# Four pairs of k-tiles by seven products instead of three in a decoder block's gate/up groups, with the quarters on GpSimd's queue

## The chip, the cores and the metric

The kernel runs on one core of a Trainium2 chip. The metric is the device time of one execution in microseconds, the median of several runs.

## The reference

A block of 256 tokens and width 2048, in float32: a feed-forward half step, a mixer (gated DeltaNet beside stick-breaking attention), a second feed-forward half step, a gated input embedding, and a last norm.

```python
def swiglu(x, w_gu, w_down):
    gate, up = jnp.split(x @ w_gu, 2, axis=-1)
    return (jax.nn.silu(gate) * up) @ w_down

h = h + 0.5 * swiglu(rms_norm(h, ffn1_norm[i]), ffn1_w_gu[i], ffn1_w_down[i])   # D_FF = 5632
h = h + hybrid_mixer(rms_norm(h, mix_norm[i]), ...)
h = h + 0.5 * swiglu(rms_norm(h, ffn2_norm[i]), ffn2_w_gu[i], ffn2_w_down[i])
gate = jax.nn.sigmoid(rms_norm(h, ple_norm[i]) @ ple_w_gate[i])
h = h + gate * (p[i] @ ple_w_proj[i])
return rms_norm(h, final_norm)
```

## The kernel before

Every product of two float32 matrices is made of three matmuls: each operand is split into a high part (`xh`, `whi`) and a rest (`xl`, `wlo`), and xh whi + xh wlo + xl whi go into one PSUM bank. Weights come in pairs of k-tiles, 128 x 1024 values a load (`raw`). ScalarE casts `raw` to `whi`, VectorE subtracts to get `wlo`. `next_weights` splits two pairs and up to two sums ahead of use.

A feed-forward block (`ffn`) has 11 gate/up groups, each of 512 gate and 512 up columns over 16 k-tiles (8 pairs of k-tiles for each of two column blocks b, two token tiles t). After groups 3, 7 and 11 of them two down groups follow (of two column blocks each); these three stretches are the parts. A group's matmuls are of two kinds:

- Plain steps: one pair of k-tiles of one column block, 2 k-tiles x 2 token tiles x 3 = 12 matmuls.
- Seven products in the way of Strassen and Winograd. They take `ns` pairs of k-tiles of both column blocks together. Done plainly, one pair of k-tiles takes 2 x 12 = 24 matmuls; by seven products it takes 7 x 3 = 21. The weights of these k-tiles are the quarters `R` (k-tile j of every pair, column block b), 128 x 512 ns values each. Sums of them are built as they are used: ScalarE casts the present sum to `shi`, VectorE subtracts to `slo` (two buffers of each). The next sum is made by VectorE (two additions into `R` a group) or by an accumulating DMA from GpSimd's queue (two a group). The activations' own sums and their split (`S`, `Sh`, `Sl`) are made by `halves`, a pass for two pairs of k-tiles.

The first gate/up groups of a block (two in the first, one in the second) have plain steps alone. In all others `NS` = 3, and `NS_DOWN` = 2, 3, 3 for the three parts' down groups.

`plan` writes the order out: while a group's plain steps run, the seven products of the group behind it (its follower) stand between them at the steps `at`, in other PSUM banks, and the quarters of the group two further on are loaded into the buffers that the follower's sums set free:

```python
at = [first + j * (n_plain - 1 - first) // 7 for j in range(7)]
...
for x, one in zip((5, 6, 7, 7), after.loads()):
    loads.setdefault(at[x] if x < 7 else min(at[6] + 1, n_plain - 1), []).append(one)
```

All loads are issued on SP's queue, in the order of the plan, so one that waits for its buffer holds those behind it. At the end of a gate/up group VectorE multiplies (`sil`), transposes 32 x 32 blocks (`tb`), and `transposed` sends them through DRAM (`scr`) to `tT`, from which `hTh` and `hTl` are made. `lanes` advance such work by one `yield` at every plain step. A scheduler then fixes each engine's instruction order at build time.

Of the kernel before, what the change touches and what calls it, by code (L numbers as in the profile page):

```python
# [10 lines left out]
F32 = mybir.dt.float32  # L11
F32R = mybir.dt.float32r
# [4 lines left out]
P = 128  # L17
T = 256
# [11 lines left out]
NS = 3  # L30
# [11 lines left out]
def block_kernel(ctx, tc, a, out):  # L42
# [156 lines left out]
    def norm_block(nT, which, j, tmp):  # L199

        if j < 3:
            lanes.add(0, norm_block_behind(nT, which, j, tmp))
            return
# [39 lines left out]
    class Group:  # L243
# [24 lines left out]
        def load(self, j, b):  # L268

            self.raw[j, b] = raw = current[0].tile([P, NS, NB], F32, tag=f"R{j}{b}", name="R")[:, 0:self.ns]  # L270
            nc.sync.dma_start(out=raw, in_=self.quarters[b][j])
# [61 lines left out]
    def plan(n):  # L333
# [24 lines left out]
        made = []  # L358
        for i, group in enumerate(groups):
# [29 lines left out]
    for nb in range(3):  # L389
        order += [("pair", a["w_pp"][nb])] + [("pair", a["w_pg"][nb][g]) for g in range(KD // 2)]  # L390
    order.append(("pair", a["w_pp"][3]))

    def halves(kind, his, los, ns, wait=0):
# [5 lines left out]
        sh = fp.tile([P, 4, NS, P], F32R, tag="Sh", name="Sh")  # L399
        sl = fp.tile([P, 4, NS, P], F32R, tag="Sl", name="Sl")  # L400
        for g0 in range(0, ns, 2):
            n = min(2, ns - g0)
            hi, lo = his[g0 // 2], los[g0 // 2]
            x = fp.tile([P, 2, 4, P], F32, tag="tT", name="tT").rearrange("p t q y -> p (t q y)")[:, 0:2 * n * T]
            nc.vector.tensor_tensor(out=x, in0=hi[:, 0:2 * n].bitcast(F32).rearrange("p k x -> p (k x)"),
                                    in1=lo[:, 0:2 * n].bitcast(F32).rearrange("p k x -> p (k x)"), op=ALU.add)
            x = x.rearrange("p (g j t y) -> p g j t y", g=n, j=2, t=2)
            a11, a12, a21, a22 = (x[:, :, j, t, :] for t in range(2) for j in range(2))
# [870 lines left out]
```

## Time and profile before

| | us |
|---|---|
| runs | 1960.52, 1960.58, 1961.28 (median 1960.58) |
| the profiled execution | 1958.5 |
| its span | 1956.8 |
| TensorE, VectorE, ScalarE, GpSimd busy | 1939.7, 1536.0, 1153.7, 83.9 |

The profile is one execution; its span is what the hardware profiler saw of the program, and the execution's own time is a little longer. Matmuls overlap, and their ends are modelled, so how much TensorE does in a stretch is read from the distance between the starts of its matmuls. In rows of groups, "busy, mean ns of one | idle before" are given, with what ended that idle time.

### The profile page before, as it was taken

To read this page: it belongs to the slowest core of one execution; us is meant where nothing else is said; L and a number is where in the kernel's file an instruction comes from. 1 tells how busy PE (TensorE), PEld (TensorE's weight loads), DVE (VectorE), ACT (ScalarE), POOL (GpSimd) and SP (SyncE) were. 2 spreads that over 40 slices of the span, in tenths; PEclk is the share of its full clock that TensorE was granted. 3 is DMA by queue.
4 is the path that set the end of the run, shared out by engine and by line. 5 is a ranking of instruction groups with operands and counts; after the bars stand their busy time and mean duration, and the time that the engine had idled before them with its cause. 6 is when DMAs were issued, how large, how long until landed. Compare 5 with 4: busy or idle time off the path is not lost.

```text
span 1956.8 us, 24735 instructions
## 1 busy us (share of the span) xinstructions
PE 1939.7 (99%) x8945; PEld 1606.5 (82%) x8945; DVE 1536.0 (78%) x1771; ACT 1153.7 (59%) x1402; POOL 83.9 (4%) x108
## 2 busy tenths in 40 slices
PE   9999999999999999999999999999999999999998
PEld 7887888888888888878788888888888888888887
DVE  6889778897788766797856678888879887798755
ACT  7655656566565567664555465665566555665554
POOL 0000000000000000010100000000000000000000
PEclk9999999999999999999999999999999999999999
DMA  8988888888888765556555788887888878887764
GB/s 316 296 238 255 265 275 243 261 257 260 264 254 256 222 209 165 174 169 213 178 195 160 243 289 243 253 270 242 250 265 281 281 223 247 261 271 239 236 207 147
DMA packets 164379, 468.28 MB, mean 239 GB/s; under 512 B 20641, under 2 KB 59553, under 8 KB 164129
## 3 DMA queue, kind: packets, MB, share of 16 engines
q1 hardware_dynamic: 154176, 418.57, 62.1%
q0 software_dynamic: 8928, 46.67, 13.6%
q8 instruction: 70, 1.15, 0.2%
q10 hardware_dynamic: 1152, 1.47, 0.2%
q14 instruction: 53, 0.43, 0.1%
HBM read 444.62 MB, written 22.02 MB: 238 GB/s over the span
## 4 chain that ended last, share of the span: by engine, by line
PE 90%; DVE 5%; issue 3%; DMA 1%; ACT 1%; POOL 0%; SPq 0%; ACTq 0%; POOLq 0%; DVEq 0%
PE u L481 6%; PE u L482 6%; PE u L480 5%; PE g L480 5%; PE g L482 5%; PE g L481 5%; PE d L480 5%; PE d L482 5%; PE d L481 5%; PE pj L108 3%; PE pj L109 3%; PE pj L107 3%; PE g L316 3%; PE g L318 3%; PE g L317 3%
## 5 line engine op out<-in xcount | busy, mean ns | idle before, releaser
L72 ACT CAST whi<-raw 128x1024 fp32r<-128x1024 f32 (+1 forms) x531 | 557.0, 1051 | 525.3 <-PE d L482 113.6
L73 DVE TENSOR_TENSOR wlo<-raw,whi 128x1024 fp32r<-128x1024 f32 (+1 forms) x531 | 643.2, 1216 | 217.9 <-ACT whi L72 212.5
L285 DVE TENSOR_TENSOR slo<-R,shi 128x1536 fp32r<-128x1536 f32 (+1 forms) x217 | 365.6, 1686 | 125.1 <-ACT shi L284 123.5
L284 ACT CAST shi<-R 128x1536 fp32r<-128x1536 f32 (+1 forms) x217 | 309.7, 1428 | 158.6 <-PE g L318 50.6
L481 PE MATMUL u<-wlo,nTh 128*128 128x512 f32 x476 | 185.3, 389 | 0.2 <-DVE wlo L73 0.2
L481 PE MATMUL g<-wlo,nTh 128*128 128x512 f32 x476 | 185.4, 390 | 0.0
L482 PE MATMUL g<-whi,nTl 128*128 128x512 f32 x476 | 185.3, 389 | 0.0
L482 PE MATMUL u<-whi,nTl 128*128 128x512 f32 x476 | 185.2, 389 | 0.0
L480 PE MATMUL u<-whi,nTh 128*128 128x512 f32 x476 | 184.9, 389 | 0.0
L480 PE MATMUL g<-whi,nTh 128*128 128x512 f32 x476 | 184.3, 389 | 0.3 <-ACT whi L72 0.3
L107 PE MATMUL pj<-whi,nTh 128*128 128x512 f32 x448 | 179.6, 401 | 0.0
L108 PE MATMUL pj<-wlo,nTh 128*128 128x512 f32 x448 | 175.3, 391 | 2.2 <-DVE wlo L73 2.2
L109 PE MATMUL pj<-whi,nTl 128*128 128x512 f32 x448 | 174.9, 390 | 0.0
L481 PE MATMUL d<-wlo,hTh 128*128 128x512 f32 x448 | 174.3, 389 | 0.0
L480 PE MATMUL d<-whi,hTh 128*128 128x512 f32 x448 | 174.3, 389 | 0.0
L482 PE MATMUL d<-whi,hTl 128*128 128x512 f32 x448 | 174.3, 389 | 0.0
L289 DVE TENSOR_TENSOR R<-R 128x1536 f32<-128x1536 f32 (+1 forms) x62 | 104.4, 1684 | 0.9
L481 PEld LDWEIGHTS u<-wlo,nTh 128*128 128x128 f32 x476 | 89.3, 188 | 19.1 <-DVE wlo L73 0.7
L481 PEld LDWEIGHTS g<-wlo,nTh 128*128 128x128 f32 x476 | 89.4, 188 | 19.0 <-DVE wlo L73 0.4
L480 PEld LDWEIGHTS g<-whi,nTh 128*128 128x128 f32 x476 | 89.3, 188 | 18.9 <-ACT whi L72 0.5
L482 PEld LDWEIGHTS u<-whi,nTl 128*128 128x128 f32 x476 | 89.4, 188 | 18.6
L480 PEld LDWEIGHTS u<-whi,nTh 128*128 128x128 f32 x476 | 89.3, 188 | 18.6
(304 smaller groups left out, 3223.8 us busy)
## 6 DMA issues: line engine op xcount, KB each, us to landing
raw<-in_w_gu SPq DMA_DIRECT2D x237, 512.0 KB, 5.5
raw<-in_w_down SPq DMA_DIRECT2D x112, 512.0 KB, 5.2
raw<-in_w_in SPq DMA_DIRECT2D x112, 512.0 KB, 3.5
R<-in_w_gu2q SPq DMA_DIRECT2D x40, 768.0 KB, 5.9
R<-in_w_gu1q SPq DMA_DIRECT2D x36, 768.0 KB, 5.9
scr<-tb SPq DMA_DIRECT2D x74, 256.0 KB, 4.8
raw<-in_w_out SPq DMA_DIRECT2D x32, 512.0 KB, 4.6
raw<-in_w_pg SPq DMA_DIRECT2D x32, 512.0 KB, 4.1
```

The costliest lines, as they stand in the source:

```text
L72: nc.scalar.copy(hi[:, j, :], raw[:, j, :])
L73: nc.vector.tensor_tensor(out=lo[:, j, :], in0=raw[:, j, :], in1=hi[:, j, :], op=ALU.subtract)
L107: nc.tensor.matmul(outs[t], xh[:, c], whi[:, j, :], start=st, stop=False)
L108: nc.tensor.matmul(outs[t], xh[:, c], wlo[:, j, :], start=False, stop=False)
L109: nc.tensor.matmul(outs[t], xl[:, c], whi[:, j, :], start=False, stop=sp)
L284: nc.scalar.copy(hi, w)
L285: nc.vector.tensor_tensor(out=lo, in0=w, in1=hi, op=ALU.subtract)
L289: nc.vector.tensor_tensor(out=self.raw[x], in0=self.raw[x], in1=self.raw[y], op=ALU.add)
L316: nc.tensor.matmul(out, xh, whi[:, g, :], start=st, stop=False, skip_group_check=True)
L480: nc.tensor.matmul(out, xh[:, c], whi[:, j, :], start=st, stop=False, skip_group_check=True)
L481: nc.tensor.matmul(out, xh[:, c], wlo[:, j, :], start=False, stop=False, skip_group_check=True)
L482: nc.tensor.matmul(out, xl[:, c], whi[:, j, :], start=False, stop=sp, skip_group_check=True)
```

## The change

`NS` goes from 3 to 4: a gate/up group with products now has 8 plain steps instead of 10, and seven products of 12 matmuls instead of 9. The quarters grow from 768 to 1024 KB, and with them every cast, split, addition and accumulation of a gate/up sum. The down groups keep 2, 3, 3.

- `at` puts the products into neighbouring steps, from step 1 (gate/up after gate/up) or 2, and lets them pile up in the last step where a group has too few.
- The quarters of the group two further on are loaded from GpSimd's queue, in another order (the one that the first sum reads comes first, the last one in the next group's first step), each into the buffer that is free first. Only the first group's loads of a block stay on SP.
- `halves` works in place in the buffer of `sil`; a gate/up group has two passes of two pairs instead of one of two and one of one.
- The gated block goes through DRAM as one write of 512 KB and four reads in runs of 1 KB (two writes and four reads in runs of 512 B before), with more plain steps between write, reads and use.
- At a block's end the norm's blocks alternate between two lanes and two buffers.
- The input embedding is loaded and split in the last stage instead of ahead of the second feed-forward block, and its weights `w_pp` come after `w_pg`.

```diff
-NS = 3
+NS = 4
...
-            self.raw[j, b] = raw = current[0].tile([P, NS, NB], F32, tag=f"R{j}{b}", name="R")[:, 0:self.ns]
-            nc.sync.dma_start(out=raw, in_=self.quarters[b][j])
-
-        def loads(self):
-            return [("load", lambda j=j, b=b: self.load(j, b)) for j, b in ((0, 1), (1, 0), (0, 0), (1, 1))]
+            self.raw[j, b] = raw = current[0].tile([P, NS, NB], F32, tag=self.home[j, b], name="R")[:, 0:self.ns]
+            self.queue.dma_start(out=raw, in_=self.quarters[b][j])
+
+        def loads(self, last=None):
+            free = [last.home[q] for q in ((0, 1), (1, 0), (0, 0), (1, 1))] if last else ["R0", "R1", "R2", "R3"]
+            self.queue = nc.gpsimd if last else nc.sync
+            use = (0, 0), (0, 1), (1, 1), (1, 0)
+            self.home = dict(zip(use, free))
+            return [("load", lambda q=q: self.load(*q)) for q in use]
...
-            at, loads = [], {}
+            at, loads, carried = [], {0: carried}, []
             if follower is not None and follower.ns:
-                first = 2 if group.ns else 8
-                at = [first + j * (n_plain - 1 - first) // 7 for j in range(7)]
+                first = 8 if not group.ns else 1 if group.kind == follower.kind else 2
+                at = [min(first + j, n_plain - 1) for j in range(7)]
...
-                    for x, one in zip((5, 6, 7, 7), after.loads()):
-                        loads.setdefault(at[x] if x < 7 else min(at[6] + 1, n_plain - 1), []).append(one)
+                    *three, last = after.loads(follower)
+                    for x, one in zip((4, 5, 6), three):
+                        loads.setdefault(at[x], []).append(one)
+                    carried = [last]
...
-        order += [("pair", a["w_pp"][nb])] + [("pair", a["w_pg"][nb][g]) for g in range(KD // 2)]
+        order += [("pair", a["w_pg"][nb][g]) for g in range(KD // 2)] + [("pair", a["w_pp"][nb])]
...
-            x = fp.tile([P, 2, 4, P], F32, tag="tT", name="tT").rearrange("p t q y -> p (t q y)")[:, 0:2 * n * T]
+            x = fp.tile([P, 2 * NB], F32, tag="sil", name="S")[:, 0:n * NB]
...
-            def down_input(u, sil, th, tl):
+            def down_input(u, sil, th, tl, landing, back):
...
-                tT = fp.tile([P, 2, 4, P], F32, tag="tT", name="tT")
-                yield from transposed(lambda t: sil[:, t, :], tT)
+                tb = fp.tile([P, 4, 2, P], F32, tag="tT", name="tb")
+                for t in range(2):
+                    nc.vector.transpose(tb[:, :, t].rearrange("p c (j x) -> p c j x", j=4),
+                                        sil[:, t, :].rearrange("p (j c x) -> p c j x", j=4, c=4))
+                yield
+                scr = dr.tile([P, 4, 2, P], F32, tag="scr2", name="scr2", bufs=2)
+                nc.sync.dma_start(out=scr, in_=tb)
+                for _ in range(landing):
+                    yield
+                tT = fp.tile([P, 4, 2, P], F32, tag="tT", name="tT")
+                for c in range(4):
+                    nc.sync.dma_start(out=tT[32 * c:32 * c + 32].rearrange("x q t i -> x q (t i)"),
+                                      in_=scr[:, c].rearrange("(q x) t i -> x q (t i)", q=4))
+                for _ in range(back):
+                    yield
...
-                            norm_block(nxt, next_norm, nb, lambda: fp.tile([P, 2, 4, P], F32, tag="tT", name="tT"))
-                            lanes.advance(0)
+                            norm_block(nxt, next_norm, nb, lambda x=("tT", "sil")[nb % 2]:
+                                       fp.tile([P, 2, 4, P], F32, tag=x, name="tT"), nb % 2)
+                            lanes.advance(nb % 2)
```

What the scheduler makes of it, at three places. First GpSimd's queue in the first block's first part. Before, it holds the accumulations (L293) of one group after another:

```order
L293 DMA R<-in_w_gu1q 128x1536 x2
L293 DMA R<-in_w_down10q 128x1024 x4
L293 DMA R<-in_w_gu1q 128x1536 x8
L293 DMA R<-in_w_down11q 128x1536 x4
L293 DMA R<-in_w_gu1q 128x1536 x8
```

With the change the quarters' loads (L271) stand between the accumulations (L299):

```order
L299 DMA R<-in_w_gu1q 128x2048 x2
L271 DMA R<-in_w_down10q 128x1024 x4
L299 DMA R<-in_w_down10q 128x1024 x2
L271 DMA R<-in_w_down10q 128x1024 x4
L299 DMA R<-in_w_down10q 128x1024 x2
L271 DMA R<-in_w_gu1q 128x2048 x4
L299 DMA R<-in_w_gu1q 128x2048 x2
L271 DMA R<-in_w_gu1q 128x2048 x4
```

A group's four loads have come off SP's queue; they stand behind the accumulations of the group ahead of it and in front of its own.

Second VectorE from the first to the third split of a gate/up group that follows another (first block, second part). Before:

```order
L285 TENSOR_TENSOR slo<-R,shi 128x1536
L289 TENSOR_TENSOR R<-R 128x1536
L73 TENSOR_TENSOR wlo<-raw,whi 128x1024
L285 TENSOR_TENSOR slo<-R,shi 128x1536
L435 SCALAR_TENSOR_TENSOR sil<-u_3527,rstd_517,sil 128x512
L435 SCALAR_TENSOR_TENSOR sil<-u_3528,rstd_517,sil 128x512
L73 TENSOR_TENSOR wlo<-raw,whi 128x1024
L167 STREAM_TRANSPOSE tb<-sil 128x512 x2
L73 TENSOR_TENSOR wlo<-raw,whi 128x1024
L289 TENSOR_TENSOR R<-R 128x1536
L73 TENSOR_TENSOR wlo<-raw,whi 128x1024 x2
L285 TENSOR_TENSOR slo<-R,shi 128x1536
```

With the change:

```order
L291 TENSOR_TENSOR slo<-R,shi 128x2048
L445 SCALAR_TENSOR_TENSOR sil<-u_3429,rstd_515,sil 128x512
L295 TENSOR_TENSOR R<-R 128x2048
L445 SCALAR_TENSOR_TENSOR sil<-u_3430,rstd_515,sil 128x512
L73 TENSOR_TENSOR wlo<-raw,whi 128x1024
L452 STREAM_TRANSPOSE tb<-sil 128x4x128
L291 TENSOR_TENSOR slo<-R,shi 128x2048
L452 STREAM_TRANSPOSE tb<-sil 128x4x128
L295 TENSOR_TENSOR R<-R 128x2048
L73 TENSOR_TENSOR wlo<-raw,whi 128x1024 x2
L291 TENSOR_TENSOR slo<-R,shi 128x2048
```

The sums are wider, and three splits of pairs stand between the first and the third instead of five; the gating has come in between as before.

Third VectorE at the end of the first block's first part, where down goes over to gate/up and the halves of the gate/up activations are made. Before, from the first to the second pass:

```order
L289 TENSOR_TENSOR R<-R 128x1536
L414 TENSOR_TENSOR Sl<-S,Sh 128x4x256
L73 TENSOR_TENSOR wlo<-raw,whi 128x1024
L285 TENSOR_TENSOR slo<-R,shi 128x1536
L412 TENSOR_TENSOR S<-tT 128x128
L289 TENSOR_TENSOR R<-R 128x1536
L412 TENSOR_TENSOR S<-S,tT 128x128
L412 TENSOR_TENSOR S<-tT 128x128
L412 TENSOR_TENSOR S<-S,tT 128x128
L73 TENSOR_TENSOR wlo<-raw,whi 128x1024 x2
L414 TENSOR_TENSOR Sl<-S,Sh 128x4x128
L285 TENSOR_TENSOR slo<-R,shi 128x1536
```

With the change, the second pass:

```order
L295 TENSOR_TENSOR R<-R 128x2048
L431 TENSOR_TENSOR S<-S 128x2x128
L73 TENSOR_TENSOR wlo<-raw,whi 128x1024
L431 TENSOR_TENSOR S<-S 128x2x128
L73 TENSOR_TENSOR wlo<-raw,whi 128x1024
L431 TENSOR_TENSOR S<-S 128x2x128
L291 TENSOR_TENSOR slo<-R,shi 128x2048
L431 TENSOR_TENSOR S<-S 128x2x128
L516 SCALAR_TENSOR_TENSOR h<-d_1315,h 128x512
L516 SCALAR_TENSOR_TENSOR h<-d_1316,h 128x512
L73 TENSOR_TENSOR wlo<-raw,whi 128x1024
L434 TENSOR_TENSOR Sl<-S,Sh 128x1024
```

The second pass is as wide as the first, and the update of h has come in ahead of its end.

More of the change, by code (lines that the diff above doesn't have):

```diff
@@ L197, in norm_block_behind, with norm_block @@
                 yield
-    def norm_block(nT, which, j, tmp):
+    def norm_block(nT, which, j, tmp, lane=0):
         if j < 3:
-            lanes.add(0, norm_block_behind(nT, which, j, tmp))
+            lanes.add(lane, norm_block_behind(nT, which, j, tmp))
             return
@@ L357, in plan @@
             groups[0].plain.sort(key=lambda x: x[1])
-        made = []
+        made, carried = [], []
         for i, group in enumerate(groups):
@@ L509, in ffn @@
                         hTl.append(tl)
-                        gen = down_input(outs, sil, th, tl)
+                        i0, i1 = PARTS[group.part]
+                        last = len(hTh) == i1
+                        gen = down_input(outs, sil, th, tl, 2, (3 if i1 - i0 == 4 else 2) if last else 4)
                         next(gen)
                         lanes.add(0, gen)
-                        if len(hTh) == PARTS[group.part][1]:
+                        if last:
+                            lanes.advance(0)
                             lanes.advance(0)
```

57 lines of the change are left out of this document (30 added, 27 removed).

## The prediction

> **What bounds the kernel now.** I read the page's first part, then TensorE's own waits, then its spacing, since a kernel whose TensorE never waits is paid in matmuls.
>
> ```profile
> span 1956.8 us, 24735 instructions
> PE 1939.7 (99%) x8945; PEld 1606.5 (82%) x8945; DVE 1536.0 (78%) x1771; ACT 1153.7 (59%) x1402; POOL 83.9 (4%) x108
> ```
>
> ```profile
> PE pj L108 <- DVE wlo L73: 2.2, 4, 1.1
> PE u L316 <- ACT Sh L413: 1.3, 2, 0.9
> ```
>
> The page alone does not prove that TensorE is the bound, because the ends of its matmuls are modelled. Its waits do: their two largest rows (total, times, longest) are 2.2 and 1.3 us in a whole execution. The second one lies inside the feed-forward blocks, at the step from a part's down groups to the next gate/up group. What a matmul costs is the spacing of their starts. These are the first and the last of 32 neighbours ahead of that wait:
>
> ```profile
> 181.74 0.39 PE L481 MATMUL d<-wlo,hTh 128*128 128x512 f32 x1
> ...
> 188.76 0.39 PE L482 MATMUL d<-whi,hTl 128*128 128x512 f32 x1
> 190.04 0.50 PE L316 MATMUL u<-shi,Sh 128*128 128x512 f32 x1 [0.89 <-ACT Sh L413]
> ```
>
> (188.76 - 181.74)/31 = 0.2265 us a matmul, and then 0.89 us of waiting. VectorE is the engine next to the bound. The windows (length, then busy time and count of PE, PEld, DVE, ACT, POOL, then clock, DMA share, GB/s) hold one gate/up stretch (264 to 305.5), the two stretches with the wait, and one with much traffic:
>
> ```profile
> 150.00:200.00 50.00, 49.09 (x216) 39.90 (x215) 45.14 (x50) 30.83 (x34) 2.62 (x3) 1.00 0.81 243
> 264.00:305.50 41.50, 41.50 (x185) 34.37 (x184) 33.46 (x29) 25.07 (x26) 1.75 (x2) 1.00 0.86 268
> 1300.00:1350.00 50.00, 49.58 (x218) 40.29 (x217) 45.57 (x50) 30.96 (x34) 2.59 (x3) 1.00 0.81 246
> ```
>
> ```profile
> 200.00:250.00 50.00, 50.00 (x222) 41.40 (x221) 38.48 (x32) 30.10 (x29) 1.75 (x2) 1.00 0.86 282
> ```
>
> The granted clock is 1.00 in all of them. VectorE is busy 81% of a gate/up stretch, and 90% and 91% where TensorE loses 0.9 and 0.4 us.
>
> **TensorE.** Taking one more pair of k-tiles through the products replaces 2 plain steps of 12 matmuls (24) by 3 more matmuls in each of 7 products (21). That holds for 9 + 10 = 19 gate/up groups, so 19 x 3 = 57 matmuls go: 57 x 0.2265 = 12.9 us. All of it lies on the path. The down groups keep their numbers.
>
> **VectorE and ScalarE.** What the splits, sums and halves cost is in the groups by form:
>
> ```profile
> L73 DVE TENSOR_TENSOR wlo<-raw,whi 128x1024 fp32r<-128x1024 f32 x529 | 641.8, 1218 | 216.4 <-ACT whi L72 211.2 <-DMA tT<-scr 1.5 <-DMA raw<-in_w_down 1.5
> L285 DVE TENSOR_TENSOR slo<-R,shi 128x1536 fp32r<-128x1536 f32 x189 | 331.6, 1755 | 121.5 <-ACT shi L284 121.1
> L289 DVE TENSOR_TENSOR R<-R 128x1536 f32<-128x1536 f32 x54 | 94.7, 1753 | 0.8
> L285 DVE TENSOR_TENSOR slo<-R,shi 128x1024 fp32r<-128x1024 f32 x28 | 34.0, 1221 | 3.7 <-ACT shi L284 2.4
> ...
> L491 DVE SCALAR_TENSOR_TENSOR h<-d,h 128x512 f32<-128x512 f32 x48 | 31.1, 682 | 3.5 <-PE d L482 3.5
> L435 DVE SCALAR_TENSOR_TENSOR sil<-u,rstd,sil 128x512 f32<-128x512 f32 x44 | 30.9, 743 | 0.0
> L167 DVE STREAM_TRANSPOSE tb<-sil 128x512 f32<-128x512 f32 x44 | 28.6, 686 | 0.0
> L444 DVE TENSOR_TENSOR hTl<-tT,hTh 128x512 fp32r<-128x512 f32 x44 | 28.3, 684 | 0.0
> L324 DVE TENSOR_TENSOR g<-g,part 128x512 f32<-128x512 f32 x38 | 26.3, 693 | 3.5 <-ACT part L323 3.5
> ...
> L414 DVE TENSOR_TENSOR Sl<-S,Sh 128x1024 fp32r<-128x1024 f32 x12 | 14.6, 1220 | 1.4 <-ACT Sh L413 1.4
> ...
> L412 DVE TENSOR_TENSOR S<-S,tT 128x256 f32<-128x256 f32 x24 | 10.0, 417 | 0.1
> ...
> L405 DVE TENSOR_TENSOR tT<-nTh,nTl 128x1024 f32<-128x1024 f32 x6 | 7.3, 1224 | 0.2
> ...
> L414 DVE TENSOR_TENSOR Sl<-S,Sh 128x512 fp32r<-128x512 f32 x10 | 6.8, 682 | 0.0
> L412 DVE TENSOR_TENSOR S<-S,tT 128x128 f32<-128x128 f32 x20 | 5.7, 283 | 0.0
> ...
> L405 DVE TENSOR_TENSOR tT<-nTh,nTl 128x512 f32<-128x512 f32 x6 | 4.1, 684 | 0.0
> ```
>
> ```profile
> L284 ACT CAST shi<-R 128x1536 fp32r<-128x1536 f32 x189 | 280.4, 1484 | 152.4 <-PE g L318 48.6 <-DVE R L289 37.3 <-PE d L318 21.9
> L284 ACT CAST shi<-R 128x1024 fp32r<-128x1024 f32 x28 | 29.3, 1056 | 6.2 <-PE d L318 4.3 <-PE g L318 2.0
> ```
>
> 512 columns more cost 1755 - 1221 = 0.534 us on VectorE and 1484 - 1056 = 0.428 on ScalarE, so a split of 2048 columns is estimated at 2.29 us, its cast at 1.91, and an addition R at 2.29. Three rows cost 0.69: the additions in PSUM (L324), the transposes and the splits of the gated block; h costs 0.68.
>
> Gate/up following gate/up (13 stretches), before: 10 pairs x 1.218 + 7 splits x 1.755 + 2 additions R x 1.753 + 4 x 0.69 in PSUM + 2 x 0.743 for the gating + 4 x 0.69 for its transposes and splits = 35.0 us, while TensorE takes 183 x 0.2265 = 41.4. The window's 33.5 confirms it (neighbours overlap a little). After: 8 x 1.218 + 9 x 2.29 + 7.0 = 37.4 us against 180 x 0.2265 = 40.8, that is 92% instead of 84%. TensorE still covers it.
>
> Down to gate/up at the second part (two stretches, one in each block), before: 12.2 + 12.3 + 3.5 + 2.8 + 2.7 for h + 6.6 for the halves (one pass of 1.22 + 4 x 0.417 + 1.22 = 4.1, one of 0.68 + 4 x 0.283 + 0.68 = 2.5) = 40.1 against 41.4. After, with both halves' passes at 4.1: 46.5 against 204 x 0.2265 = 46.2. At the first part (two stretches, 8 plain steps): 37.6 against 36.0 before, 44.1 against 40.8 after. This is where TensorE lost the 0.9 and 0.4 us. The excess doubles from 1.6 to 3.3 us, but the products now stand in steps 2 to 7 instead of 2, 2, 3, 4, 4, 5, 6: the one that waited for the halves comes a plain step (2.7 us) later. Bounds: from -1.3 (both waits vanish) to +3.4 (each grows by the 1.7 us more). I take 0, since the later step and the larger excess nearly cancel. For the two second-part stretches I take 0.3 us each, with 0 and 0.9 (the nearest wait that the trace has) as ends: 0.6.
>
> Elsewhere the lead of the splits over the products decides. A split in a gate/up stretch, and the first product matmul that reads it:
>
> ```profile
> 448.20 1.76 DVE L285 TENSOR_TENSOR slo<-R,shi 128x1536 fp32r<-128x1536 f32 x1 [0.56 <-ACT shi L284]
> ```
>
> ```profile
> 453.22 0.39 PE L317 MATMUL g<-slo,nTh 128*128 128x512 f32 x1
> ```
>
> It is ready 3.3 us ahead (453.22 - 449.96). There are two buffers, so a cast starts when the product two before it ends. From there to its own product are now 3 more matmuls (0.68 us), and cast and split take 0.43 + 0.53 longer: the lead falls by 0.3 to 3.0 us. So no wait in the steady stretch: 0, with 0 to 0.4 each as bounds (0 to 5.2). The place with the smallest lead is the first block's third product, where the sums begin:
>
> ```profile
> 68.76 1.76 DVE L285 TENSOR_TENSOR slo<-R,shi 128x1536 fp32r<-128x1536 f32 x1 [1.60 <-ACT shi L284]
> ```
>
> ```profile
> 70.83 0.39 PE L317 MATMUL g<-slo,Sh 128*128 128x512 f32 x1
> ```
>
> Its lead is 0.3 us (70.83 - 70.52). Three sums of 2048 columns take 3 x 0.96 + 2 x 0.53 = 3.9 us more, and two longer products give back 1.4, so the worst is 2.2. The quarter that the first sum reads is now loaded first instead of third, which can cancel it. Between 0 and 2.2 I take 0.7.
>
> **Transfers.** The queues, the issues and SP's waits:
>
> ```profile
> q1 hardware_dynamic: 154176, 418.57, 62.1%
> q0 software_dynamic: 8928, 46.67, 13.6%
> ```
>
> ```profile
> R<-in_w_gu2q SPq DMA_DIRECT2D x40, 768.0 KB, 5.9
> R<-in_w_gu2q POOLq DMA_DIRECT2D x20, 768.0 KB, 8.3
> ```
>
> ```profile
> SPq L271 <- DVE slo L285: 293.4, 111, 4.8
> ```
>
> ```profile
> L293 POOL DMA_DIRECT2D R<-in_w_gu2q x20: 862/865/947, 1175.1 to 1709.4; - x20
> ```
>
> SP sat 293 us behind quarters whose buffers were not free, and the pairs behind them in its queue sat too. 116 quarters leave it for GpSimd's queue, which now holds four loads and two accumulations for each group, 6 x 0.87 = 5.2 us of issuing in 40.8. SP's gain is worth nothing now, as none of TensorE's waits above ends with a transfer. On GpSimd's queue the accumulations now stand behind quarters that wait for a buffer; each of these buffers is freed by a split that precedes the accumulation's own cause on VectorE, so nothing is held: 0. An accumulation of 1 MB should land after 8.3 x 4/3 = 11 us; three products, 16.3 us, lie between its issue and its use.
>
> The gated block's way through DRAM becomes one write and four reads instead of two and four, with pieces twice as long, and has two steps more. It is read only by the last four plain steps of the down group: 0. The input embedding's split (one 512-column cast and subtraction) moves to the last stage, where VectorE is the less loaded:
>
> ```profile
> 1850.00:1900.00 50.00, 49.59 (x219) 40.73 (x219) 29.71 (x36) 26.92 (x36) 0.71 (x1) 1.00 0.65 217
> ```
>
> 30 of 50 us: 0, and putting w_pg ahead of w_pp gives at most the 0.4 us lost here.
>
> **Sum.** The profiled execution took 1958.5 us, a span of 1956.8 and 1.7 around it; the median of the three runs, 1960.6, is 2.1 higher. 1956.8 - 12.9 + 0.6 + 0.7 = 1945.2 of span, 1946.9 for that execution, 1949 against the median.
>
> **The skill's rules on the queue.** On GpSimd's queue a byte takes twice SP's time: 13.6% of 1956.8 us for 46.67 MB is 5.70 us per MB, against 2.90 on q1. But all of q0's transfers accumulate, so the trace cannot tell the queue from the addition; that is a rival below. The Trainium skill (DMA: Bandwidth & Descriptors, "Issuing engines are not separate DMA queues") says that transfers of all issuing engines run on the same 16 DMA engines and interleave. By that rule plain quarters keep q1's price and the sum stays 1949; no run here shows it yet. The skill's SBUF — State Buffer ("SBUF: two separate sides") speaks against the move: GpSimd cannot write descriptors while VectorE runs in a two-port mode. The row above bears on that: 20 issues beside a VectorE that was busy four fifths of the time took 862 to 947 ns, so nothing was starved. What the page's rule would do here, late quarters, is part of the second rival.
>
> **Rivals.** (1) The first three sums of a group hang on one another (cast, split, addition, split, addition, split) and become the pace of gate/up stretches. In VectorE's order before, the way from the first cast to the end of the third split is 1.48 + 3 x 1.755 + 2 x 1.753 + 5 pairs x 1.218 + 2.9 for the gating = 19.2 us. From the end of the product that frees the first buffer to the third product, TensorE then gives 111 matmuls, 25.1 us. After, it is 1.91 + 5 x 2.29 + 3 x 1.218 + 2.9 = 19.9 us against 96 matmuls, 21.7: a slack of 1.8 us instead of 5.9. Handoffs such as the 0.56 us ahead of the split quoted above can eat it. If four of them do and each of the 13 stretches loses 0.5 to 1.5 us beyond: 1956 to 1969, middle 1962, no gain. Against it: neighbours overlap a little, as the window showed, and the second and third casts lie under pairs and gating in VectorE's order.
>
> (2) Slower: plain quarters cost q0's price. A gate/up stretch then needs 5.24 MB x 2.90 + 2.10 x 5.70 + 4.19 x 5.70 = 51 us of the DMA engines in 40.8, 10 us over, 13 times: about 2080. With q1's price it is 39.4, so it decides from 3.2 us per MB on. For it: q0's price. Against it: 282 GB/s, as much as the new stretch needs (11.5 MB in 40.8 us), passed in 200 to 250 at a share of 0.86, and an accumulation also reads what it adds to.
>
> (3) The waits at the first parts vanish and nothing new comes: 1949 less 0.6, 0.7 and 1.3 is 1946.4.
>
> **Numbers.** Forecast, with rival 3 as its lower end: 0.70, its own range 1946 to 1954. Rival 1: 0.18, half of it within 0.2% of the time before. Rival 2, wholly or in part: 0.08. Something else: 0.04. No change means within 0.2% of 1960.6 (3.9 us, about what a measurement tells from none): below 1956.7 is faster. Faster 0.78, same 0.12, slower 0.10. The range runs from 1946 to 1958, into rival 1.
>
> **What would show it.** TensorE's waits stay under 6 us in total and its spacing at 0.2265. VectorE is at 88 to 92% of gate/up windows. Splits lead their products by about 3 us, with the least at a group's third. Quarters from GpSimd land within 10 us, and the DMA share stays under 0.97. I am wrong if TensorE waits for slo or shi in every gate/up stretch (rival 1), or if shi waits for R's transfers (rival 2).

## The result and the profile after

The changed kernel is slower: 1.0124 times the time before (95% interval 1.0104 to 1.0144). Executions took 1984.0, 1984.3 and 1988.2 us against a median of 1960.9 in the same comparison; one more, at a granted clock of 0.85 throughout, took 2146 us and is left out. The profiled execution is the slowest of the three, 1988.2 us. Its page begins:

```profile
span 1986.4 us, 24346 instructions
PE 1944.1 (98%) x8888; PEld 1597.1 (80%) x8888; DVE 1585.7 (80%) x1733; ACT 1162.3 (59%) x1364; POOL 147.0 (7%) x224
```

The 57 matmuls are gone (8945 to 8888), yet the span grew by 29.6 us. The starts of TensorE's matmuls tell where (us from one stage's first matmul to the next's):

| | before | after | difference |
|---|---|---|---|
| first feed-forward block | 696.0 | 709.1 | +13.1 |
| mixer | 461.1 | 466.9 | +5.9 |
| second feed-forward block | 688.9 | 698.4 | +9.4 |
| last stage | 100.3 | 101.6 | +1.3 |

In the two feed-forward blocks 57 x 0.2265 = 12.9 us went. Against that, steps from one matmul to the next that were more than 0.25 us too long cost 21.9 us more than before (24.3 against 2.3), steps at half the granted clock 8.2, steps 0.02 to 0.25 us too long 4.2, and the rest 1.1. That makes 35.4 - 12.9 = +22.5. The waits (total, times, longest), with ScalarE's and VectorE's for the gated block:

```profile
ACT hTh L468 <- DMA tT<-scr: 47.2, 13, 9.6
...
DVE hTl L469 <- ACT hTh L468: 38.6, 7, 8.4
...
PE g L323 <- DVE slo L291: 10.9, 7, 1.8
...
PE g L322 <- ACT shi L290: 6.3, 3, 3.4
...
PE pj L108 <- DVE wlo L73: 2.8, 5, 1.1
PE abT L786 <- issue: 2.7, 1, 2.7
```

The first of them stood in the profile before too, at a twentieth:

```profile
ACT hTh L443 <- DMA tT<-scr: 2.3, 6, 0.9
```

The chain of waits around the longest stall (start, us, what; the first product matmul stood at 543.42) shows how a read of the gated block reaches TensorE:

```profile
519.15 0.63 DVE tb L452
519.80 7.40 DMA scr<-tb
527.21 0.33 SPq L461
...
528.58 11.79 DMA tT<-scr
...
540.96 0.61 ACT hTh L468
541.57 1.81 ACT shi L290
...
543.40 2.30 DVE slo L291
...
545.75 0.79 PE g L323
```

Nothing that TensorE does there needs `hTh`. But ScalarE works in order, and its casts `hTh` stand ahead of the cast `shi` of the group's fifth sum. ScalarE's rows at that place:

```profile
529.81 1.04 ACT L72 CAST whi<-raw 128x1024 fp32r<-128x1024 f32 x1
540.43 1.14 ACT L468 CAST hTh<-tT 128x512 fp32r<-128x512 f32 x2 [9.58 <-DMA tT<-scr]
541.48 1.89 ACT L290 CAST shi<-R 128x2048 fp32r<-128x2048 f32 x1
```

TensorE then waits twice, for the cast and for the split, and runs at half its clock. This happens at the fifth product of seven gate/up groups:

```profile
543.42 0.50 PE L322 MATMUL g<-shi,nTh 128*128 128x512 f32 x1 [3.36 <-ACT shi L290]
545.75 0.79 PE L323 MATMUL g<-slo,nTh 128*128 128x512 f32 x1 [1.82 <-DVE slo L291]
546.34 0.63 PE L324 MATMUL g<-shi,nTl 128*128 128x512 f32 x1
546.77 0.63 PE L322 MATMUL g<-shi,nTh 128*128 128x512 f32 x1
```

(546.77 - 546.34 = 0.43 us between starts instead of 0.2265.) The windows, in the columns of the prediction's:

```profile
264.00:305.50 41.50, 40.17 (x177) 32.95 (x176) 34.64 (x27) 25.10 (x23) 3.60 (x6) 1.00 0.88 278
500.00:550.00 50.00, 44.82 (x188) 36.41 (x187) 36.40 (x28) 26.13 (x24) 3.96 (x6) 0.94 0.74 231
...
1500.00:1550.00 50.00, 48.33 (x201) 38.91 (x202) 45.68 (x47) 31.46 (x34) 4.43 (x7) 0.94 0.77 235
```

Why the reads land late is the issue order of two queues. The accumulation of a group's second sum went out at 526.72, the four reads from 527.21 on. Their time to landing, there:

```profile
L461 SPq DMA_DIRECT2D tT<-scr x4: 326/454/928, 527.2 to 528.6; - x4
...
DMA to landing us min/median/max: 3.5/10.8/12.0
```

The first of the four still landed after 3.5 us. At the six other stalls the accumulation went out 0.2 to 1.2 us after the first read, and the last read, or the last two, landed after 8.9 to 11.7 us. What the DMA engines did meanwhile is in the trace's packets. The accumulation (queue q0) is 128 packets of 8 KB, a read (q1) 128 packets of 1 KB. The next lines (packets, MB, share of 16 engines) hold first those that started from 530.3 to 532.3 us, when three reads were waiting, then those from 532.3 to 535:

```profile
q0 software_dynamic: 47, 0.39, 93.8%
```

```profile
q0 software_dynamic: 65, 0.53, 94.5%
q1 hardware_dynamic: 64, 0.07, 8.9%
```

At first packets of the accumulation went alone; why is open. Then the two took turns, one packet each: 16 and 16 in every 0.66 us, of which a packet of the accumulation took 0.63 and one of the read 0.06. At that rate a read's 128 packets last as long as the accumulation's 128. The last two reads landed 3.8 and 4.1 us after the accumulation (536.26), beside the next quarter, which GpSimd's queue had issued at 531.09 and which landed at 539.87.

All 88 reads of the gated block, sorted by what was in flight: 38 were issued behind an accumulation and landed after 8.2 us in the median (longest 12.0), 31 ahead of one after 2.9, and 19 with none in flight after 2.9. Before, no read was issued behind an accumulation, 58 stood ahead of one (3.9, longest 5.7).

### The profile page after: what moved, and what is told of

Its sections match the earlier page's. It is cut to its first block, busy times and chain, and to the rows that moved or that the text cites. A ratio compares the mean times of both kernels' runs of the same rounds, so it can differ in the third digit from the quotient of the medians.

```text
span 1986.4 us, 24346 instructions
## 1 busy us (share of the span) xinstructions
PE 1944.1 (98%) x8888; PEld 1597.1 (80%) x8888; DVE 1585.7 (80%) x1733; ACT 1162.3 (59%) x1364; POOL 147.0 (7%) x224
## 4 chain that ended last, share of the span: by engine, by line
PE 70%; DVE 11%; DMA 8%; issue 7%; ACT 3%; SPq 1%; POOL 0%; ACTq 0%; POOLq 0%; DVEq 0%
PE d L506 4%; PE d L507 4%; PE d L505 4%; PE u L506 3%; PE u L507 3%; PE u L505 3%; DMA tT<-scr 3%; PE pj L108 3%; PE pj L109 3%; PE pj L107 3%; DVE wlo L73 3%; PE g L323 3%; PE g L506 3%; PE g L507 3%; PE g L505 3%
## 5 line engine op out<-in xcount | busy, mean ns | idle before, releaser
L72 ACT CAST whi<-raw 128x1024 fp32r<-128x1024 f32 (+1 forms) x493 | 515.9, 1049 | 418.8 <-PE pj L109 113.8
L73 DVE TENSOR_TENSOR wlo<-raw,whi 128x1024 fp32r<-128x1024 f32 (+1 forms) x493 | 597.7, 1218 | 178.1 <-ACT whi L72 175.4
L291 DVE TENSOR_TENSOR slo<-R,shi 128x2048 fp32r<-128x2048 f32 (+2 forms) x217 | 435.6, 2011 | 100.6 <-ACT shi L290 99.2
L290 ACT CAST shi<-R 128x2048 fp32r<-128x2048 f32 (+2 forms) x217 | 366.3, 1693 | 206.4 <-DVE R L295 78.9
L295 DVE TENSOR_TENSOR R<-R 128x2048 f32<-128x2048 f32 (+2 forms) x62 | 124.3, 2004 | 0.2
L323 PE MATMUL g<-slo,nTh 128*128 128x512 f32 x228 | 91.8, 403 | 10.9 <-DVE slo L291 10.9
L108 PEld LDWEIGHTS pj<-wlo,nTh 128*128 128x128 f32 x448 | 84.5, 189 | 21.1 <-DVE wlo L73 5.0
L506 PEld LDWEIGHTS d<-wlo,hTh 128*128 128x128 f32 x448 | 84.1, 188 | 19.4 <-DVE wlo L73 1.9
L109 PEld LDWEIGHTS pj<-whi,nTl 128*128 128x128 f32 x448 | 84.5, 189 | 17.7
L107 PEld LDWEIGHTS pj<-whi,nTh 128*128 128x128 f32 x448 | 84.4, 189 | 17.6 <-ACT whi L72 1.1
```

The lines of the kernel that those rows point to most:

```text
L72: nc.scalar.copy(hi[:, j, :], raw[:, j, :])
L73: nc.vector.tensor_tensor(out=lo[:, j, :], in0=raw[:, j, :], in1=hi[:, j, :], op=ALU.subtract)
L107: nc.tensor.matmul(outs[t], xh[:, c], whi[:, j, :], start=st, stop=False)
L108: nc.tensor.matmul(outs[t], xh[:, c], wlo[:, j, :], start=False, stop=False)
L109: nc.tensor.matmul(outs[t], xl[:, c], whi[:, j, :], start=False, stop=sp)
L290: nc.scalar.copy(hi, w)
```

## The experiments

Five explanations are named in the expectations. Theory A: the quarters on GpSimd's queue hold the reads. B: the wider accumulation by itself slows every small read beside it. C: the new way through DRAM is slow. The prediction's first rival: the chain of sums. D, formed after the first four runs: the products' new places put the reads just behind the second accumulation, and such a read waits for that transfer's end. Each run below has its median and its ratio to the kernel before, which took 1960.7 to 1961.7 us (median) in the five comparisons. Kernels of different comparisons are compared by their ratios, times 1961 us: the changed kernel's 1.0124 stands for 1985.5 us, the mean of its three executions.

**The quarters back on SyncE's queue.**

```diff
-            self.queue = nc.gpsimd if last else nc.sync
+            self.queue = nc.sync
```

> The changed kernel with all plain quarters back on SyncE's queue; the order on the other engines stays as in the changed kernel. Theory A (quarters on GpSimd's queue, beside its accumulations, keep the gated block's four small reads from landing; ScalarE stands at the casts hTh and the cast of the group's fifth sum behind them comes late): the reads land 4 to 7 us after issue, ScalarE waits under 10 us in all for them (47 us in the changed kernel), TensorE's waits for shi and slo in gate/up groups go from 17 to under 3 us, no drop of the granted clock, 1947 to 1956 us. Rival B (the wider accumulations alone, 1 MB instead of 768 KB, delay the reads): as many stalls as now, 1978 to 1988. Rival C (the new way through DRAM, one write and four reads, is slow by itself): 1978 to 1988 as well. If SyncE's queue now stands behind quarters whose buffers are not free, the reads behind them start late: 1955 to 1970, with ScalarE's wait still at hTh.

1979.7 us, ratio 1.0095 (1.0080 to 1.0109). The reads are nearly as late, 35 of them behind an accumulation with a median of 9.1 us, and ScalarE waits almost as long:

```profile
ACT hTh L468 <- DMA tT<-scr: 45.8, 12, 7.6
```

Theory A falls as the main cause: the queue holds 0.0029 x 1961 = 5.7 us, hardly more than the interval, and not 25. The longest wait fell from 9.6 to 7.6 us, and no read behind a group's second gate/up accumulation took over 9.9 us (12.0 in the changed kernel). That fits the quarter which followed on the accumulation's queue at the place shown. This run also prices a plain byte on GpSimd's queue. The queues here and in the changed kernel (packets, MB, share of the span of 16 engines):

```profile
q0 software_dynamic: 8928, 56.63, 15.8%
```

```profile
q1 hardware_dynamic: 117568, 313.70, 45.9%
q0 software_dynamic: 25632, 161.49, 30.1%
```

Accumulations alone are 15.8% of 1977.5 us for 56.63 MB, 5.5 us per MB; the 104.86 MB more of the changed kernel took 0.301 x 1986.4 - 312.4 = 285.5 us, 2.7 per MB.

**Quarters in runs of 2 KB**, in loads and accumulations alike:

```diff
-    m[name + "q"] = np.ascontiguousarray(b[:, :ns].transpose(0, 3, 2, 1, 4))
+    m[name + "q"] = np.ascontiguousarray(b[:, :ns].transpose(0, 3, 1, 2, 4))
...
-            self.queue.dma_start(out=raw, in_=self.quarters[b][j])
+            self.queue.dma_start(out=raw, in_=self.quarters[b][j].rearrange("g p n -> p g n"))
```

> The changed kernel with the quarters laid out in DRAM so that a partition's 8 KB come as four runs of 2 KB, for plain loads and accumulations alike; queues and order unchanged. Theory A in the form that the length of the neighbour's packets matters (a small read waits for one long packet on each DMA engine): the reads land within 7 us, ScalarE waits under 15 us for them, 1950 to 1962 us. Theory A in the form that the bytes in flight matter, not their packets: the reads stay at 8 to 13 us and the time at 1980 to 1990. Rivals B and C: 1980 to 1990.

2008.6 us, ratio 1.0231 (1.0207 to 1.0255): worse, which no theory expected. An accumulation takes longer to issue (1.31 us instead of 0.88) and to land (10.9 instead of 8.8 in the median), so more reads are issued behind one, 73 of 88, with a median of 6.9 us. The packets still took turns: from 546 to 549 us 237 of the accumulation's queue started, now 2 KB long, and 216 of the reads' queue (26 of all under 512 B). There four reads landed 1.8 to 2.1 us apart, after the first had taken 6.2. So shorter runs do let a read past faster, and the median fell; but twice as many reads came to stand behind an accumulation.

**The casts behind.** ScalarE's and VectorE's order alone is changed: an edge, which fixes the order at build time and adds no wait, puts `hTh` and `hTl` behind the newest cast `shi` and split `slo`:

```diff
-                    nc.scalar.copy(hi, tv)
-                    nc.vector.tensor_tensor(out=lo, in0=tv, in1=hi, op=ALU.subtract)
+                    behind = newest if back == 4 and newest[0] else None
+                    with tc.issue_after(behind[0].ins) if behind else nullcontext():
+                        nc.scalar.copy(hi, tv)
+                    with tc.issue_after(behind[1].ins) if behind else nullcontext():
+                        nc.vector.tensor_tensor(out=lo, in0=tv, in1=hi, op=ALU.subtract)
```

> The changed kernel in which the casts hTh and splits hTl of a gated block that is not a part's last are queued behind the newest cast shi and split slo that the program has emitted by then; queues and transfers unchanged. If late reads do harm only through the order on ScalarE (theory A, and rivals B and C too): the reads still land 8 to 13 us after issue where they collide, TensorE's waits for shi and slo in gate/up groups fall under 4 us, no clock drop in the feed-forward blocks, 1948 to 1957 us. If the chain of sums or VectorE at 92% is the cause (the first rival of the prediction): little changes, 1975 to 1990, with TensorE still waiting at the fifth product.

1964.0 us, 1.0012 (1.0003 to 1.0021). 22 reads still land late (median 8.7), and TensorE's waits for shi and slo are 3.1 us instead of 17.7, nearly all of them at one place, where four loads of `raw` stand behind the late reads. The time is above the range that was expected (1948 to 1957), since the mixer's loss stays (466.8 us) and one drop of the clock is left in the feed-forward blocks. By the ratios 22 us come through the order on ScalarE, with VectorE's behind it, and the first rival falls: the same sums, at the same places, keep up. (Fewer reads are late here than in the changed kernel, 22 against 38, so a part of the 22 us may be theirs.)

**The kernel before with GpSimd's queue.** `nc.gpsimd` for all quarters but those of each block's first sum group.

> The kernel before with only its quarters (all but the first sum group's) moved to GpSimd's queue: three pairs, the old way of the gated block, the old order. Theory A: the gated block's reads land later than the 4.5 to 7.1 us of before and ScalarE waits more than 2.3 us for them, 1962 to 1980 us if the order behind them is as tight as in the changed kernel, 1960 if it is not. Rivals B and C: no difference, 1959 to 1962.

1967.6 us, 1.0025 (1.0012 to 1.0037), but not by the reads: one of 124 was issued behind an accumulation, and ScalarE's wait for them is 1.6 us. ScalarE's waits for the quarters themselves rise from 22 to 38.5 us in all, the largest row being

```profile
ACT shi L285 <- DMA R<-in_w_gu1q: 9.5, 4, 5.5
```

Whether they make the 5 us is not shown; the run's profile is of its fastest execution, 1963.2 us.

**The old way through DRAM.** `tb`, the one write and the four reads give place to the lines before:

```diff
+                tT = fp.tile([P, 2, 4, P], F32, tag="tT", name="tT")
+                yield from transposed(lambda t: sil[:, t, :], tT)
```

> The changed kernel with the gated block's old way through DRAM (two writes of 256 KB, four reads in 512-byte runs, its old steps); four pairs, GpSimd's queue for the quarters, and ScalarE's order with the casts hTh ahead of the fifth sum's cast stay. Theory D (the last reads of a block are issued within about 1 us of the second accumulation and land only with it, 10 us later; it is a matter of tenths of a microsecond between two issues): the reads now start 2 us or more ahead of the accumulation or well behind it, land in 4 to 7 us, ScalarE waits under 10 us for them, 1955 to 1966 us. Rival B (the 1 MB accumulation slows any small read that runs beside it): reads of 8 us and more, 1975 to 1988.

2018.0 us, 1.0279 (1.0253 to 1.0305). The expectation of D missed: the old way does not bring the reads ahead, 47 stand behind an accumulation and ScalarE waits 92.4 us. Rival C falls, since the new way is better than the old one at these places; what is left are B and the places of the products.

**The products by the old rule.**

```diff
-                first = 8 if not group.ns else 1 if group.kind == follower.kind else 2
-                at = [min(first + j, n_plain - 1) for j in range(7)]
+                first = 2 if group.ns else 8
+                at = [first + j * (n_plain - 1 - first) // 7 for j in range(7)]
```

> The changed kernel with its products put back by the old rule (after plain steps 2, 2, 3, 4, 4, 5, 6 of 8 instead of 1 to 7); all else stays. Theory D: the second accumulation is issued later than the gated block's reads, they land in 4 to 7 us, and ScalarE's order has the casts hTh behind the fifth sum's cast: no stall at the fifth product. Then 1952 to 1964 us. Against it stands the chain of sums (the prediction's first rival): with two pairs of products in neighbouring places the splits may not keep up, TensorE waits for slo at the second and fifth products of each group, 1965 to 1985.

1961.3 us, 0.9996 (0.9986 to 1.0006): 25 us less. Accumulations go out 3 to 5 us after the first read starts, and four reads are left behind one. 53 are ahead; their median of 5.8 us is longer than the 2.9 of the changed kernel, but in the median 3.8 of it had passed when the accumulation went out. The places change ScalarE's order too, so this run alone does not tell which of the two it was. The waits:

```profile
ACT hTh L468 <- DMA tT<-scr: 1.2, 2, 0.7
PE g L323 <- DVE slo L291: 0.8, 2, 0.5
```

**A short second accumulation**, which separates D from B and from all else that the places change:

```diff
-                nc.gpsimd.dma_start(out=self.raw[x], in_=self.quarters[y[1]][y[0]], accum_op=ALU.add)
+                nc.gpsimd.dma_start(out=self.raw[x][:, 0:n], in_=self.quarters[y[1]][y[0]][:, 0:n], accum_op=ALU.add)
...
-                    add_loaded((0, 0), (1, 0))
+                    add_loaded((0, 0), (1, 0), 1)
```

> The changed kernel in which each group's second accumulation moves only one pair of k-tiles (256 KB of 1 MB in gate/up); the rest of that sum is left out. Order, queues, issue times and sums stay. Theory D in the form that a read issued just behind an accumulation waits for that transfer to end: the reads land in 4 to 6 us where they took 10 to 13, ScalarE's 47 us of waiting at hTh fall under 15, the stalls at the fifth product go (20 us and about 9 us of halved clock), and the mixer's loss stays: 1958 to 1969 us. If the reads are late for another reason (the first accumulation, the quarter that follows, the new way): reads still 8 us and more, 1978 to 1987.

This kernel leaves out a part of each such sum; it serves to time the transfer. 1961.3 us, 0.9995 (0.9983 to 1.0007), again 25 us less. As in the changed kernel, 15 reads were issued behind a second gate/up accumulation: they landed after 4.1 us in the median (longest 5.7) instead of 9.4 (12.0). The 22 behind a group's first accumulation, which is whole, still took 7.4 (23 and 8.1 in the changed kernel). ScalarE's waits fell from 47.2 to 17.6 us, a little short of the 15 expected, and the stalls at the fifth product are gone. At the place shown above, with the accumulation 0.4 us ahead of the reads (0.5 in the changed kernel):

```profile
DMA to landing us min/median/max: 3.3/4.8/5.6
```

Issue order and the length of the transfer in front make the delay; that is shown. B, that every small read beside 1 MB is slow, falls by the changed kernel itself: its 31 reads that were issued ahead of an accumulation took 2.9 us in the median (four at one place 7.5 to 10.1).

**The norm blocks on one lane.**

```diff
-                            norm_block(nxt, next_norm, nb, lambda x=("tT", "sil")[nb % 2]:
-                                       fp.tile([P, 2, 4, P], F32, tag=x, name="tT"), nb % 2)
-                            lanes.advance(nb % 2)
+                            norm_block(nxt, next_norm, nb, lambda: fp.tile([P, 2, 4, P], F32, tag="tT", name="tT"))
+                            lanes.advance(0)
```

> The changed kernel with only the norm blocks at the end of each feed-forward block put back on one lane and one buffer. From the first projection matmul to the second block's first the changed kernel takes 466.9 us, the kernel before 461.1, with the same 2360 matmuls. If the second lane causes that (the last norm blocks' activations and the mixer's small loads come late on ScalarE): 460.5 to 462.5 here, the last stage 100.3 to 101.0 instead of 101.6, and 1977 to 1982 us. If it comes from elsewhere: 466 to 467.5 and 1983 to 1987.

1969.7 us, 1.0039 (1.0026 to 1.0052), below the 1977 to 1982 expected. The mixer takes 461.0, as expected of the lane, and the last stage 99.7, a little less. In the changed kernel ScalarE's table load and the cast `ea` had come ahead of the casts `wpad` for which the mixer's first `abT` waits:

```profile
722.47 1.28 ACT L814 ACT_TABLE_LOAD   x1
726.92 0.21 ACT L814 ACTIVATE ea<-alog 128x8 f32<-128x8 f32 x1 [3.17 <-DMA alog<-in_a_log]
727.36 0.52 ACT L790 CAST wpad<-wabr 128x16 fp32r<-128x16 f32 x4 [0.24 <-DMA wabr<-in_w_ab]
```

The other 9.8 us of this profile's gain fell in the feed-forward blocks (705.7 and 692.0). As many reads are behind (38) and ScalarE waits as long for them (45.8 us), but TensorE waits for shi and slo 14.7 us instead of 17.7, and two drops of the clock are left there instead of three. That was not expected; what each late read costs varies, and why the lane changes it is not shown.

**The repairs together.** Casts behind and one lane:

> The casts behind (as in the kernel with that edit alone, 1964.0 us) and the norm blocks on one lane together. If the two losses are independent: 1964.0 less 5 to 7, so 1956 to 1960 us, with the mixer at 460.5 to 462.5. If the mixer's loss comes from elsewhere: 1962 to 1966.

1956.2 us, 0.9970 (0.9959 to 0.9981): the losses add. Old rule and one lane:

> The changed kernel with two edits: its products by the old rule (1961.3 us alone) and the norm blocks on one lane. If the two losses add up, the mixer falls from 466.9 to 461 to 462 us and the last stage from 101.6 to 99.7, so 1961.3 - 7 = 1954 us, 1952 to 1957. If the old rule's gain and the lane's overlap (the lane alone gave 16 us, more than its 7 in the mixer and the last stage): 1957 to 1962.

1954.4 us, 0.9959 (0.9946 to 0.9973). With the casts behind as third edit:

> As the kernel with the products by the old rule and one lane, and the casts hTh queued behind the newest cast shi besides. The old rule's order has these casts behind the fifth sum already and TensorE waits for no split there, so the third edit should bring nothing: within 2 us of that kernel. Should the reads, which then land in 4 to 8 us, still hold ScalarE, it is 2 to 4 us faster.

1953.6 us, 0.9957 (0.9942 to 0.9971): nothing more, as expected. And `NS = 3` in the second of these:

> The kernel with the products by the old rule and one lane, with three pairs instead of four; everything else of the change stays. It prices the fourth pair alone: 57 matmuls x 0.2265 = 12.9 us. If that gain arrives whole: 12 to 14 us slower than with four pairs, 1965 to 1970. If the wider sums eat part of it: nearer, 1956 to 1964. If the change's other parts had gains of their own, it would end under the 1961 of the kernel before.

1960.6 us, 0.9993 (0.9983 to 1.0003). The fourth pair is worth 1960.6 - 1954.4 = 6.2 us here, half of its matmuls, as the second branch of the expectation has it.

**The same on SyncE's queue.** Old rule and one lane, with `self.queue = nc.sync`:

> Four pairs, products by the old rule, norm blocks on one lane, and the quarters on SyncE's queue again. Moving the quarters to GpSimd's queue alone cost the kernel before 5 to 6 us, and taking them back gave the changed kernel 6.6. If that price holds wherever the reads land well: 1954.4 - 5 = 1949 us, 1946 to 1951. If it was only another form of the same collision: 1953 to 1956, no change.

1950.3 us, 0.9945 (0.9931 to 0.9960), the fastest kernel here, 10 us under the one before. Its waits and a gate/up window:

```profile
ACT hTh L468 <- DMA tT<-scr: 3.5, 3, 1.4
PE pj L108 <- DVE wlo L73: 2.2, 4, 1.1
PE u L323 <- DVE slo L291: 0.5, 1, 0.5
```

```profile
264.00:305.50 41.50, 41.50 (x185) 34.34 (x184) 36.34 (x29) 26.45 (x24) 1.75 (x2) 1.00 0.90 282
```

With the casts behind besides:

> The same with the casts hTh queued behind the newest cast shi besides. If the queue has a price of its own: 1947 to 1950 us. If not: 1952 to 1955.

1950.9 us, 0.9947 (0.9933 to 0.9962). With three pairs:

> Three pairs, products by the old rule, one lane, quarters on SyncE's queue: all that is left of the change is the block's way through DRAM, the order of loads and the last stage's order. With GpSimd's queue it took 1960.6. If the queue's price is 5 us with three pairs too: 1955 to 1957, and the fourth pair is then worth what separates this from the four-pair kernel of this call: 6 us as on GpSimd's queue, or 12.9 if the queue had eaten the rest. If the queue costs nothing here: 1959 to 1962.

1959.7 us, 0.9993 (0.9984 to 1.0001). The new places with casts behind:

> The changed kernel's places for the products, casts hTh behind, one lane, quarters on SyncE's queue. With GpSimd's queue it took 1956.2. If the queue has a price of its own: 1949 to 1952 us. If not: 1955 to 1958.

1952.5 us, 0.9956 (0.9940 to 0.9971). By the ratios GpSimd's queue costs four pairs 2.0 to 2.7 us in the three comparisons (2.8 to 4.1 by the medians), each less than its own interval of about 4 us, and three pairs nothing. The last two times with four pairs lie just above the ranges that were expected of a price. So a small price is likely with four pairs, and not shown. On SyncE's queue the fourth pair is worth 1959.7 - 1950.3 = 9.4 us; with intervals of about 3 us this is not clearly more than the 6.2 on GpSimd's.

## Why the prediction was wrong, point by point

- **TensorE, -12.9: right in number, not in reach.** 57 matmuls went. Where nothing else is in the way, 9.4 us of it arrive. The missing 3.5 would fit the prediction's bounds for the steady stretches (0 to 5.2), where it took 0, but only 2.0 of them are found: in the two feed-forward blocks of the best kernel, steps 0.02 to 0.25 us too long sum to 5.8 us against 3.8 with three pairs.
- **Down to gate/up: inside its bounds.** The waits of 0.9 and 0.4 us at the first parts are gone, which is the lower bound of -1.3 where it took 0; one of 0.40 stands at a second part (0.6 forecast).
- **Leads: right where they were worked out.** The split that the prediction quotes is that of a sixth product; where nothing holds it, it leads by 2.98 us (forecast 3.0). A third product that follows gate/up has 2.8 or 3.9 us instead of 4.2, and 0.06 at two places. "The least at a group's third" holds at those two; where the casts `hTh` wait, the fifth has 0.05. VectorE's 88 to 92% of a gate/up window comes true once the stalls are gone (36.34 of 41.5).
- **The first sums, +0.7**: waits of 0.54, 0.18 and 1.01 us at 65 to 80 us, 1.7 in all, inside its bounds. But the 0.54 stands at the second product and the other two at plain steps, not at the third product, so the size is luck.
- **The gated block, 0: the step that failed.** "It is read only by the last four plain steps of the down group" names who reads the data, not who stands behind the instruction that waits for it. ScalarE's casts `hTh` wait for the reads, the fifth sum's cast stands behind them, and TensorE behind that: 22 us by the run with the casts behind, a part of it the clock's.
- **Transfers, "nothing is held: 0": failed too.** It asked whether accumulations wait for buffers, not what stands behind an accumulation on the DMA engines. The places of the products moved that accumulation, from 2.3 us and more after the first read to between 0.5 us ahead of it and 1.2 us after it at the seven stalls. The old places took 25 us off, and so did the short accumulation: these are no further microseconds, but the 22 seen from the other end of the chain.
- **The norm blocks' lanes, no term at all**: 5.9 us in the mixer and 1.9 in the last stage, by the run that undid them.
- **The clock, no term**: after the long stalls 8.2 us in the feed-forward blocks, a part of the same 25.
- **Rival 1** fell, by the run with the casts behind. Its sign, TensorE waiting for slo or shi, came in seven gate/up groups, so the sign could not tell it from this cause.
- **Rival 2** said slower, and slower it is, but not for its reason: plain quarters cost 2.7 us per MB, below its deciding 3.2. Here the trace agrees with the Trainium skill (DMA: Bandwidth & Descriptors, "Issuing engines are not separate DMA queues") in the price per byte. Still, moving the quarters cost the kernel before 5 us and the changed kernel about 6, by the ratios. The rule on GpSimd and VectorE's two-port mode that the prediction cites from the Trainium skill (SBUF — State Buffer, "SBUF: two separate sides") shows in no issue: the accumulations' took 0.87 to 1.05 us (0.86 to 0.95 before), the plain quarters' 0.53 to 0.58.

With the old places and one lane the kernel stands at 0.9959 x 1960.6 = 1952.6 us, 3.6 above the forecast of 1949; the other 33 us of the miss are the late reads and the lanes. That the best kernel's 1950.3 lies beside 1949 does not bear the prediction out: it is another kernel, with the places, the lane and the queue of before.

## What to carry to other kernels

A moved transfer is priced by what waits behind it, first on its own queue, then on every engine whose next instruction needs it, down to what stands behind that instruction in order; who reads the data in the end says nothing of it. A lead of tenths of a microsecond between issues on two queues is not to be relied on: the stalls came with an accumulation from 0.5 us ahead of the first read to 1.2 us after it. Place a small, waited-for read well ahead of a long transfer, or put the instruction that waits for it behind the critical ones. Each part of a change that touches another stage gets its own term.

## What the runs showed of the hardware

- A 128 KB read issued behind a 1 MB accumulation lands about when that transfer does (8.2 us in the median against 2.9), and issued ahead of it mostly does not wait. By the trace's packets the two take turns, a 1 KB packet (0.06 us) against an 8 KB packet (0.63 us), and with runs of 2 KB a 1 KB packet against a 2 KB one; so a small read in short packets pays for as many of the long ones. The Trainium skill (DMA: Bandwidth & Descriptors, "Queues, rings and completion order") says that a DMA engine changes between rings only after a whole packet. The turns agree with it if its packet is what the trace calls one, which no run shows; an engine's share of the accumulation (128 packets over 16 engines) is not sent in one turn here.
- Half the granted clock followed waits much shorter than the stretch it lasted: after 2.67 us for `abT`, and in two experiments (2 KB runs; old places and one lane) after single waits of 1.82 and 1.93, each time for 3.4 us by the trace's clock record (6.8 after 3.36 + 1.82). Not always: with the quarters on SyncE's queue, waits of 1.83 and 2.37 left the clock whole. The Trainium skill (TensorE: Matmul & The Clock Gate, "What's actually happening") has the half rate follow an idle window of about 3.4 us. The length of the stretch agrees; the wait ahead of it was shorter here.
